# The last modulation's loads and additions at other places within the chunks of the feed-forward

## The chip, the core and the metric

The kernel runs on one core of a Trainium2 chip. Its engines work side by side, each through its own queue of instructions: TensorE (PE in the profile, its weight loads PEld), VectorE (DVE), ScalarE (ACT), GpSimd (POOL) and SyncE (SP), which only starts DMA transfers. The metric is the time of one execution on the device in microseconds (us), as the median of several runs; lower is better.

## The reference

One layer of a diffusion step, for 128 context tokens and 256 latent tokens of width 2048. What bears on the change is the modulation and the feed-forward at the end:

```python
mod = jax.nn.silu(cond) @ lw['w_ada'] + lw['b_ada']
sh1, sc1, ga1, sh2, sc2, ga2 = [m[:, None, :] for m in jnp.split(mod, N_MOD, axis=-1)]
...
x = x + ga1 * rmsnorm(m, lw['norm_post_mix'])
h = rmsnorm(x, lw['norm_pre_ffn']) * (1.0 + sc2) + sh2
ff = (jax.nn.silu(h @ lw['w_ffn_gate']) * (h @ lw['w_ffn_up'])) @ lw['w_ffn_down']
x = x + ga2 * rmsnorm(ff, lw['norm_post_ffn'])
```

`w_ada` has 2048 x 12288 elements, six modulations of 2048 columns. The change concerns the sixth, `ga2`, which is only needed at the very end, for the last line. There are two conditions, one for the context tokens and one for the latent tokens, so each modulation is a product of two vectors with a matrix. The feed-forward has 5632 hidden columns.

## The kernel before

**Numbers.** All is float32. For a product each operand is split into a high part (`whi`, `hid_hi`, a rounded copy made by ScalarE) and a low part (`wlo`, `hid_lo`, the rest, a subtraction on VectorE), and TensorE adds three products: high by high, high by low, low by high. Every weight that comes from memory therefore costs one copy on ScalarE (L1437) and one subtraction on VectorE (L1448) of a 128 x 1024 tile before TensorE can use it.

**Chunks and steps.** The hidden columns are worked through in 11 chunks of 512 (`NFC = 11`, `FC = 4` tiles of 128). Chunk 0 is done plainly. Chunks 1 to 10 use a scheme with seven products in place of eight, for which sums of weights are formed on VectorE: a chunk's gate and up products are the kinds A to H, each in four steps i = 0 to 3 (A0 to A3, B0 to B3, and so on), and the down product of the chunk before is woven in between as DA to DH and D4 to D7. A list `steps`, written out by a loop, sets the order: A0 to A3; B0 to B3; D4; then C and E in turn, with D5, DA, DB and DC behind E0 to E3; then F and G in turn, with DE to DH behind G0 to G3; then H0 to H3, with D6 behind H0 and D7 behind H2. Every step takes one pair of split weight tiles (`whi`, `wlo`) for its matmuls (L1539) and, in `grab2`, has the pair for the third step after it made (`split_next`: the copy L1437, the sums L1420, L1444, L1445 and L1447, the subtraction L1448). There are four buffers each for `whi` and `wlo`.

**What else a step does.** `pend` is a list of small operations that the following steps put into their engines' queues: the hidden activations of the previous chunk (ScalarE's `hid_hi` and VectorE's `hid_lo`, L1630) behind A2, B0 and B2, their sums (L1637 to L1644), and the evictions of finished products. The results of the down products are added to sums in memory by transfers that GpSimd issues (L1672).

**The order.** The queues of TensorE, ScalarE, VectorE and GpSimd hold their instructions in the order in which the program calls them. SyncE's transfers in the loop are placed by a planner. An instruction waits in its queue for what it needs, and everything behind it in that queue waits too.

**The last modulation.** The generator `ada_last` computes it in four quarters `q` of 512 columns. One step of a quarter loads a tile of 128 x 512 of `w_ada` (L1476; 256 KB) into one half of a two-part buffer `w5` and lets VectorE add it, multiplied by one scalar per partition, to an accumulator, once per condition: a plain multiplication for the first tile (L1479), a multiply-add for the other fifteen (L1481). After the sixteenth step `turned` is set. Two further steps, at A0 and A1 of the next chunk, sum over the partitions with small matmuls (L1492), turn the result (L1499) and finish the quarter with three short operations on VectorE (L1502 to L1505). The generator is advanced by one step at chosen places, at the end of a step of the main loop:

```python
ada_at = ('B2', 'E0', 'E2', 'F0', 'G1', 'G3', 'H0', 'H2')
...
if (kind == "A" and i < 2) if turned[0] else c < LAST and kind + str(i) in ada_at:
    step(ada)
```

Eight places per chunk make two chunks per quarter: the 64 loads are spread over chunks 1 to 8, and chunk 9 begins with the last two steps of the fourth quarter.

Of the kernel before, what the change touches and what calls it, by code (L numbers as in the profile page):

```python
# [97 lines left out]
def tile_step(ctx: ExitStack, tc: tile.TileContext, a, o):  # L98
# [150 lines left out]
    def step(side):  # L249
        if side is not None:  # L250
            next(side, None)
# [19 lines left out]
    def paced(gen, rate):  # L271

        due = 0.0
        while True:
            due += rate[0]
            while due >= 1.0:
                due -= 1.0
                if next(gen, 1) is not None:
                    return
            yield  # L280
# [766 lines left out]
    with ExitStack() as s:  # L1047
# [84 lines left out]
        E0, S0, S12 = (pss.tile([P, 2, 3, 64], F32, tag="side", name="pst") for _ in range(3))  # L1132
# [208 lines left out]
        LAST = NFC - 1  # L1341
# [117 lines left out]
        def grab2(kept=2):  # L1459
            w = take()  # L1460
            while now:
                now.pop(0)()
            load_more(kept)
            split_next()
            return w


        d_live, turned = [0], [False]
# [50 lines left out]
        for u in range(HEAD):  # L1519
            kind, c, j = ffn_order[u]  # L1520
# [11 lines left out]
        def products(w, todo, by_tile=False):  # L1532

            order = [(x, y) for x in ((0, 1),) for y in todo] if by_tile else [((0,), y) for y in todo] + [((1,), y) for y in todo]
            for ws, (dst, stat, mov, first, last, *more) in order:
                for w_ in ws:
                    for m in range(2):
                        for x_ in range(2 - w_):
                            PE.matmul(  # L1539
                                dst, stat[x_][m], mov(w[w_], m),  # L1540
                                start=first and w_ == m == x_ == 0, stop=last and w_ == m == 1,
                                skip_group_check=any(more),
                            )
# [7 lines left out]
        def two_of(blocks, i):  # L1551
            return [[x[:, 2 * i + m, :] for m in range(2)] for x in blocks]
# [5 lines left out]
        def banks(c):  # L1558

            return dict(zip(("q2", "p2", "Q", "X", "Z"), pgu[:3] + pgu[3 + c % 2 : 4 + c % 2] + pgu[4 - c % 2 : 5 - c % 2]))  # L1560
# [13 lines left out]
        def evict(c, kind):  # L1574

            B = banks(c)
            add, mul = DVE.tensor_add, DVE.tensor_mul
            silu = lambda x, y=None: ACT.activation(x, x if y is None else y, AF.Silu)
            if kind == "A":
                now.extend([lambda: ACT.copy(sq, B["Q"]), lambda: ACT.copy(s1, B["X"])])  # L1580
            elif kind == "B":
                now.append(lambda: ACT.copy(s5, B["Z"]))
            elif kind == "C":
                now.append(lambda: silu(g0, B["Q"]))
            elif kind == "E":
                now.append(lambda: ACT.copy(e2, B["X"]))
                pend.extend([lambda: add(g1, e2, B["Z"]), lambda: silu(g1)])
            elif kind == "F":
                pend.extend([lambda: add(s5, s5, B["X"]), lambda: silu(s5)])
            elif kind == "G":  # L1590
                pend.extend([
                    lambda: add(s1, s1, B["p2"]), lambda: mul(g1, g1, s1),
                    lambda: add(sq, sq, B["q2"]), lambda: mul(g0, g0, sq),
                ])
            elif kind == "H":
                pend.append(lambda: mul(s5, s5, B["X"]))
# [67 lines left out]
        def to_sums(k, p, c):  # L1664

            u = dt["out"][turn[0] % 4]
            turn[0] += 1
            ACT.copy(u, p)  # L1668
            if c == 0:
                SP.dma_start(sums_d[k], u)  # L1670
            else:
                POOL.dma_start(sums_d[k], u, accum_op=ALU.add)  # L1672
            d_live[0] -= 1
# [11 lines left out]
        def sums_join(at):  # L1685

            for x, y in (
                ("q2", "q1"), ("q3", "q1"), ("p2", "p1"), ("p6", "p1"), ("p3", "p5"), ("p3", "p6"), ("p7", "p6"),
                ("p5", "p7"), ("p4", "p7"),
            ):  # L1690
                pend.append(lambda x=at[x], y=at[y]: DVE.tensor_add(x, x, y))
# [19 lines left out]

        rate[0] = 1.0
        ada = paced(ada_last(), rate)
        ada_at = ('B2', 'E0', 'E2', 'F0', 'G1', 'G3', 'H0', 'H2')
        pd_tiles, hid_last, x1b, done = None, None, None, 0
        d_bank, late_w = {}, []
        for kind, c, i in steps:
# [54 lines left out]
            elif kind[0] == "D":  # L1772
                w = grab2()
                while pend:
                    pend.pop(0)()
                todo = []
                for n, stat, first, last in of_d[kind]():
                    if first:
                        d_bank[n] = psm.tile([P, 512], F32, tag="mm", name="pds")
                        d_live[0] += 1  # L1780
                    todo.append((d_bank[n], stat, mov_d, first, last))
                    if last:
                        pend.append(lambda k=PROD.index(n), p=d_bank[n], c=c: to_sums(k, p, c))
                products(w, todo, by_tile=kind in ("DB", "DC"))
            else:
                w = grab2()
                if kind == "H" and i == 0:
                    while pend:
                        pend.pop(0)()
                B = banks(c)  # L1790
                products(
                    w, [(B[n], two_of(stat, i), mov_gu, first and i == 0, i == 3, not first) for n, stat, first in of_kind[kind]],
                    by_tile=(kind, i) in (("A", 3), ("B", 0), ("B", 3), ("C", 0)),
                )
                if i == 3:
                    evict(c, kind)
                if (kind, c, i) == ("C", LAST, 0):
                    sums_join(back)
                if (kind, c, i) == ("F", LAST, 0):
                    sums_rest()  # L1800
                if (kind, c, i) == ("B", LAST, 0):
                    while pend:
                        pend.pop(0)()
                    back = sums_back()
                if kind == "A" and i:
                    if c == 1 and i == 2:
                        while pend:
                            pend.pop(0)()
                        d_tiles()
                        load_more()  # L1810
                    if c == 1 and i == 2:
                        f = dt["full"]
                        pend.append(lambda: DVE.tensor_add(f, hid[0][:, :, P:T].bitcast(F32), hid[1][:, :, P:T].bitcast(F32)))
                        pend.extend(hid_sums(f[:, :, 0:P], f[:, :, P:]))
                    if i == 3 and c == 1:
                        pend.append(hid_sums_lo)
                if c > 1 and (kind, i) == ("A", 0):
                    mid = dt["out"][turn[0] % 4]
                at = kind + str(i)
                if c < LAST:  # L1820
                    if at == "H0":
                        pend.append(apart(g1, e2, g1))
                    elif at == "H1":
                        pend.append(apart(g0, sq, g0))
                if c > 1:
                    if at == "A0":
                        pend.append(apart(s5, mid, s5))
                    elif at == "A1":
                        pend.append(together(g1, e2))
                    elif at == "A2":  # L1830
                        pend.extend(hid_parts(1, e2))
                    elif at == "A3":
                        pend.append(together(g0, g1))
                    elif at == "B0":
                        pend.extend(hid_parts(0, g1))
                    elif at == "B1":
                        pend.append(together(s5, mid))
                    elif at == "B2":
                        pend.extend(hid_parts(2, mid))
                        if c < LAST:  # L1840
                            pend.extend(hid_sums(*(x.rearrange("p (j c) -> p j c", j=FC) for x in (e2, mid))))
                    elif at == "B3":
                        if c < LAST:
                            pend.append(hid_sums_lo)
                if (kind == "A" and i < 2) if turned[0] else c < LAST and kind + str(i) in ada_at:
                    step(ada)
            if (kind, c, i) == ("D", NFC - 2, 3):
                while pend:
# [174 lines left out]
```

## Time and profile before

| | |
|---|---|
| median of 3 runs | 1940.47 us (1938.39 to 1945.57) |
| the profiled execution, its own time | 1937.62 us |
| its span, from the first to the last instruction | 1935.8 us |
| feed-forward, chunks 1 to 9 (start of A0 of chunk 1 to start of A0 of chunk 10) | about 968 to 1794 us |
| granted TensorE clock, mean over the span | 0.998 |

A row of the order-of-time view gives start, length, engine, line, operation, what it writes and reads, shapes, and the count where equal neighbours are merged; in brackets stands how long the engine was idle before it and what ended that idle time. A row of the waits view reads "who waited <- for whom: us in total, times, longest". Letters such as `u`, `raw`, `dw` and `spare` are buffers. PE's instructions overlap: the length of one is more than the distance between two starts.

### The profile page before, as it was taken

The page shows a single profiled execution, that of the slowest core. Times are in us where ns is not written, and L with a number is a line of the kernel's source. Part 1 is how long each engine was busy: PE and PEld are TensorE (multiplying, and loading weights), DVE is VectorE, ACT ScalarE, POOL GpSimd, SP SyncE. Part 2 cuts the span into 40 slices and gives each one's busy share as a digit, 9 for nine tenths or more (in the row PEclk, how much of TensorE's full clock was granted, in tenths as well). Part 3 has the DMA queues.
Part 4 walks back from the last instruction along what each step waited for, and adds up shares of the span by engine and source line. Part 5 has one row for each costly group of instructions (what it writes and reads, how often), then busy time and mean ns, then how long its engine had stood idle before and what let it go on. Part 6 is the DMA issues. An engine that isn't in the chain of part 4 may idle for free.

```text
span 1935.8 us, 27972 instructions
## 1 busy us (share of the span) xinstructions
PE 1920.4 (99%) x10398; PEld 1703.5 (88%) x10398; DVE 1638.8 (85%) x2059; ACT 1069.1 (55%) x1523; POOL 145.2 (8%) x171
## 2 busy tenths in 40 slices
PE   8999999999999999999999999999999999999998
PEld 6779999999999999999988888888888888888886
DVE  5569888879776787977799999999999998998885
ACT  4233454554335655446456666666666666666554
POOL 0000000000000000003000111111111120211001
PEclk9999999999999999999999999999999999999999
DMA  9977777767754687754639596969888797969563
GB/s 390 373 261 265 232 253 226 236 220 255 257 194 142 205 285 245 220 185 158 224 102 297 122 285 152 266 161 249 195 239 208 211 236 181 247 153 253 158 204 123
DMA packets 246152, 429.12 MB, mean 222 GB/s; under 512 B 45308, under 2 KB 149948, under 8 KB 241664
## 3 DMA queue, kind: packets, MB, share of 16 engines
q1 hardware_dynamic: 199072, 386.70, 60.3%
q0 software_dynamic: 18432, 33.56, 11.1%
q10 hardware_dynamic: 28512, 7.08, 2.5%
q8 instruction: 81, 1.33, 0.3%
q14 instruction: 55, 0.45, 0.1%
HBM read 365.68 MB, written 54.53 MB: 217 GB/s over the span
## 4 chain that ended last, share of the span: by engine, by line
PE 95%; DVE 2%; DMA 2%; ACT 1%; issue 1%; SPq 0%; POOL 0%; DVEq 0%; ACTq 0%; POOLq 0%
PE pmm L257 35%; PE pgu L1539 30%; PE pdn L1539 10%; PE pds L1539 7%; PE pv L399 3%; PE pgm L382 1%; PE pf L998 1%; PE px L417 1%; PE pmm L1253 1%; PE bk L1539 1%; PE po L647 1%; PE pf L999 0%; DMA xraw<-in_w_x 0%; DMA Clo<-in_xT 0%; DMA raw<-in_w_br_gla 0%
## 5 line engine op out<-in xcount | busy, mean ns | idle before, releaser
L257 PE MATMUL pmm<-A_hi,whi 128*128 128x384 f32 x1200 | 404.3, 337 | 0.0
L257 PE MATMUL pmm<-A_hi,wlo 128*128 128x384 f32 x1200 | 401.4, 334 | 0.0
L257 PE MATMUL pmm<-A_lo,whi 128*128 128x384 f32 x1200 | 401.3, 334 | 0.0
L1437 ACT CAST whi<-u 128x1024 fp32r<-128x1024 f32 x200 | 210.1, 1055 | 179.3 <-DVE u L1444 42.3
L223 ACT CAST whi<-raw 128x1024 fp32r<-128x1024 f32 x181 | 190.3, 1054 | 185.8 <-DMA raw<-in_w_gate 54.4
L224 DVE TENSOR_TENSOR wlo<-raw,whi 128x1024 fp32r<-128x1024 f32 x179 | 218.4, 1222 | 57.4 <-ACT whi L223 57.0
L1448 DVE TENSOR_TENSOR wlo<-u,whi 128x1024 fp32r<-128x1024 f32 x200 | 242.9, 1222 | 17.9 <-ACT whi L1437 17.5
L1539 PE MATMUL pgu<-whi,A_hi 128*128 128x512 f32 x640 | 250.0, 391 | 0.0
L1539 PE MATMUL pgu<-whi,A_lo 128*128 128x512 f32 x640 | 249.2, 389 | 0.0
L257 PEld LDWEIGHTS pmm<-A_hi,whi 128*128 128x128 f32 x1200 | 225.3, 188 | 2.9 <-issue 1.4
L257 PEld LDWEIGHTS pmm<-A_lo,whi 128*128 128x128 f32 x1200 | 225.4, 188 | 0.2
L257 PEld LDWEIGHTS pmm<-A_hi,wlo 128*128 128x128 f32 x1200 | 225.2, 188 | 0.0
L574 DVE SCALAR_TENSOR_TENSOR adacc<-adaw,cond,adacc 128x1024 f32<-128x1024 f32 x180 | 222.9, 1281 | 2.7 <-DMA adaw<-in_w_ada 2.4
L1437 ACT CAST whi<-raw 128x1024 fp32r<-128x1024 f32 x157 | 165.2, 1054 | 83.0 <-PE pdn L1539 22.7
L1448 DVE TENSOR_TENSOR wlo<-raw,whi 128x1024 fp32r<-128x1024 f32 x157 | 191.8, 1222 | 8.9 <-ACT whi L1437 8.6
L1539 PE MATMUL pgu<-wlo,A_hi 128*128 128x512 f32 x640 | 185.8, 389 | 0.0
L1539 PEld LDWEIGHTS pgu<-whi,A_hi 128*128 128x128 f32 x640 | 120.1, 188 | 26.1 <-issue 0.8
L1539 PEld LDWEIGHTS pgu<-wlo,A_hi 128*128 128x128 f32 x640 | 120.2, 188 | 25.1
L1539 PEld LDWEIGHTS pgu<-whi,A_lo 128*128 128x128 f32 x640 | 120.2, 188 | 24.7
L1539 PE MATMUL pgu<-whi,S 128*128 128x512 f32 x400 | 116.6, 389 | 0.0
L1672 POOL DMA_DIRECT2D sums_d<-spare x64 | 58.6, 950 | 622.5 <-ACT spare L1668 616.1
L1539 PE MATMUL pdn<-whi,hid_lo 128*128 128x512 f32 x264 | 102.9, 390 | 0.5 <-DVE hid_lo L1630 0.5
(410 smaller groups left out, 3308.0 us busy)
## 6 DMA issues: line engine op xcount, KB each, us to landing
adaw<-in_w_ada SPq DMA_DIRECT2D x96, 512.0 KB, 4.4
raw<-in_w_d SPq DMA_DIRECT2D x70, 512.0 KB, 6.3
slab<-in_w_ada SPq DMA_DIRECT2D x32, 1024.0 KB
raw<-in_w_gate SPq DMA_DIRECT2D x64, 512.0 KB, 4.5
raw<-in_w_g SPq DMA_DIRECT2D x48, 512.0 KB, 3.7
raw<-in_w_u SPq DMA_DIRECT2D x48, 512.0 KB, 5.0
raw<-in_w_in SPq DMA_DIRECT2D x44, 512.0 KB, 4.2
u<-in_w_u SPq DMA_DIRECT2D x40, 512.0 KB, 6.1
```

The source lines that it names most:

```text
L223: ACT.copy(hi, raw)
L224: sub = lambda: eng.tensor_sub(lo, raw, hi.bitcast(F32))
L257: PE.matmul(dst, w[wi][:, k * n + n0 : k * n + n0 + P], x[xi][:, k0 + k, :], start=first and k == 0 and j == 0, stop=last and k == kts - 1 ...
L382: PE.matmul(pgv[q : q + 32, :], spad[:, k, :], slab[k // (KT // 2)][:, k % (KT // 2), :], start=k < 4, stop=k >= KT - 4,)
L399: PE.matmul(pv[2 * t + g], hT[x_][:, kb, t * P : (t + 1) * P], w_[:, g * 512 : (g + 1) * 512], start=kb == 0 and j == 0, stop=kb == KT - 1 ...
L417: PE.matmul(px, w_[:, u * P : (u + 1) * P], hT[x_][:, kb, :], start=j == 0, stop=j == 2)
L574: DVE.scalar_tensor_tensor(acc[:, c, :], w, cond[:, k, c : c + 1], acc[:, c, :], op0=ALU.mult, op1=ALU.add,)
L647: PE.matmul(dst, w[wi], x[xi], start=first and j == 0, stop=last and j == 2)
L1437: ACT.copy(hi, src)
L1448: DVE.tensor_sub(lo, src, hi.bitcast(F32))
L1539: PE.matmul(dst, stat[x_][m], mov(w[w_], m), start=first and w_ == m == x_ == 0, stop=last and w_ == m == 1, skip_group_check=any(more),)
L1672: POOL.dma_start(sums_d[k], u, accum_op=ALU.add)
```

## The change

One tuple becomes two, and the one that holds is chosen by the chunk's number: the first for chunk 1, the second for the chunks from 2 on. Each has eight places, as before.

```diff
-        ada_at = ('B2', 'E0', 'E2', 'F0', 'G1', 'G3', 'H0', 'H2')
+        ada_at = (('B0', 'B2', 'E0', 'E2', 'F0', 'G1', 'G3', 'H0'), ('A2', 'B0', 'B2', 'E0', 'E2', 'F0', 'G3', 'H1'))
...
-                if (kind == "A" and i < 2) if turned[0] else c < LAST and kind + str(i) in ada_at:
+                if (kind == "A" and i < 2) if turned[0] else c < LAST and kind + str(i) in ada_at[c > 1]:
                     step(ada)
```

In chunk 1 the place B0 is new and H2 is gone. In the later chunks A2, B0 and H1 are new, and G1, H0 and H2 are gone. The generator, its loads and its operations are the same.

## The prediction

> **What bounds the kernel now.** I read the page's head first, then the chain of waits, then the waits and the stretches of the feed-forward, and last the order of time on VectorE inside one chunk.
>
> ```profile
> span 1935.8 us, 27972 instructions
> PE 1920.4 (99%) x10398; PEld 1703.5 (88%) x10398; DVE 1638.8 (85%) x2059; ACT 1069.1 (55%) x1523; POOL 145.2 (8%) x171
> PE 95%; DVE 2%; DMA 2%; ACT 1%; issue 1%; SPq 0%; POOL 0%; DVEq 0%; ACTq 0%; POOLq 0%
> ```
>
> TensorE (PE) is busy for 99% of the span and carries 95% of the chain that ended last. The page is an average over stages, so the stage of the change has to be read alone: chunks 1 to 9 of the feed-forward, 968 to 1793 us. One row of the stretches view is one chunk (columns: length; busy time and count of PE, PEld, DVE, ACT, POOL; granted clock; DMA share; GB/s):
>
> ```profile
> 1059.70:1151.80 92.10, 91.59 (x403) 75.32 (x403) 87.02 (x91) 58.81 (x72) 11.54 (x13) 1.00 0.78 208
> 1243.90:1335.00 91.10, 91.10 (x403) 75.47 (x402) 87.06 (x91) 60.17 (x74) 14.02 (x18) 1.00 0.87 216
> 1427.20:1518.20 91.00, 91.00 (x403) 75.39 (x402) 86.22 (x90) 60.78 (x74) 14.11 (x18) 1.00 0.84 219
> ...
> PEld pdn L1539 <- DVE hid_lo L1630: 1.2, 2, 0.9
> PE pdn L1539 <- DVE hid_lo L1630: 0.5, 1, 0.5
> PEld pgu L1539 <- DVE wlo L1448: 0.2, 1, 0.2
> ```
>
> Chunks 4 and 6 hold some 402 matmuls in 91.1 us, 0.227 us each, the granted clock at 1.00 and PE busy throughout. Chunk 2 has the same count in 92.1 us. The last three rows are all that TensorE and its weight loads wait for VectorE in the stage (total, times, longest). So the stage stands at TensorE's own beat, and the only time in it that a better order on VectorE could return is the 1.0 us of chunk 2. VectorE, at 87 of 91.1 us, has little room: it is the engine that could become the bound.
>
> **The change, part by part.** No instruction is added or removed. A step is one load of 256 KB and two instructions on VectorE:
>
> ```profile
> L1481 DVE SCALAR_TENSOR_TENSOR acc<-w,cond,acc x120: 743/750/760, 1000.4 to 1701.8; 128x512 f32<-128x512 f32 x120
> L1476 SPq DMA_DIRECT2D w<-in_w_ada x64: 328/341/1746, 914.1 to 1690.1; - x64
> L1479 DVE TENSOR_SCALAR acc<-w,cond x8: 482/484/489, 992.8 to 1540.3; 128x512 f32<-128x512 f32 x8
>   DMA w<-in_w_ada: 11.3, 8
> DMA to landing us min/median/max: 2.6/5.5/11.0
> ```
>
> 64 loads and 128 instructions (120 of 750 ns, 8 of 484 ns) at eight places a chunk fill chunks 1 to 8 both before and after; chunk 9 only finishes the last quarter. In chunk 1 the place H2 goes and B0 comes. In chunks 2 to 8 the places G1, H0 and H2 go and A2, B0 and H1 come. What counts is therefore where 7 x 3 pairs of instructions stand in VectorE's order. Chunk 4, VectorE alone, at A and B (start, length, idle before):
>
> ```profile
> 1251.82 1.23 DVE L1448 TENSOR_TENSOR wlo<-u,whi 128x1024 fp32r<-128x1024 f32 x1
> 1254.51 0.69 DVE L1630 TENSOR_TENSOR hid_lo<-ep,hid_hi 128x512 fp32r<-128x512 f32 x1 [1.46 <-ACT hid_hi L1630]
> ...
> 1256.25 2.44 DVE L1448 TENSOR_TENSOR wlo<-u,whi 128x1024 fp32r<-128x1024 f32 x2
> 1260.14 0.69 DVE L1630 TENSOR_TENSOR hid_lo<-ep,hid_hi 128x512 fp32r<-128x512 f32 x1 [1.46 <-ACT hid_hi L1630]
> ...
> 1265.29 1.41 DVE L1481 SCALAR_TENSOR_TENSOR acc<-w,cond,acc 128x512 f32<-128x512 f32 x2
> 1266.62 0.69 DVE L1630 TENSOR_TENSOR hid_lo<-spare,hid_hi 128x512 fp32r<-128x512 f32 x1
> ```
>
> *A2 and B0 come.* The step at A2 ends up directly behind the weight split (L1448) that starts at 1251.82, and in front of the hid_lo at 1254.51, which belongs to A3; that at B0 stands in the same way in front of the hid_lo at 1260.14, which belongs to B1. At both places VectorE idles 1.46 us, because ScalarE's hid_hi comes late. A pair occupies 1.41 us and moves the next instruction on by 1.33 (1265.29 to 1266.62). So both pairs fit, with 0.05 to 0.13 us to spare: cost between 0 (all hidden) and 1.33 each (nothing hidden). I take 0, since the idle time is VectorE's own, and ScalarE, not VectorE, ends it. Queued behind these adds are the hid_lo of A3 and B1, and, through B1 to B3, the third hid_lo at 1266.62, for which TensorE waits:
>
> ```profile
> 1267.50 0.19 PEld L1539 LDWEIGHTS pdn<-whi,hid_lo 128*128 128x128 f32 x1
> 1296.51 0.62 PE L1539 MATMUL pds<-wlo,hid_hi 128*128 128x512 f32 x2
> 1294.25 1.23 DVE L1448 TENSOR_TENSOR wlo<-raw,whi 128x1024 fp32r<-128x1024 f32 x1
> 1306.94 0.62 PE L1539 MATMUL pgu<-wlo,A_hi 128*128 128x512 f32 x2
> 1304.72 1.22 DVE L1448 TENSOR_TENSOR wlo<-raw,whi 128x1024 fp32r<-128x1024 f32 x1
> ```
>
> These are the tight spots of chunk 4. The third hid_lo ends at 1266.62 + 0.69 = 1267.31, and its first weight load (of step D 4) starts at 1267.50: 0.19 us of margin. The wlo made in step DB ends at 1295.48 and is used three steps later, in DC, at 1296.51: 1.03. The one made in G0 ends at 1305.94 and is used in G1 at 1306.94: 1.00. If the two pairs keep to their idle time, none of these margins changes. If that cover is gone, the hid_lo in front of D 4 is late first.
>
> *G1, H0 and H2 go, H1 comes.*
>
> ```profile
> 1310.40 1.41 DVE L1481 SCALAR_TENSOR_TENSOR acc<-w,cond,acc 128x512 f32<-128x512 f32 x2
> 1327.53 1.41 DVE L1481 SCALAR_TENSOR_TENSOR acc<-w,cond,acc 128x512 f32<-128x512 f32 x2
> 1332.79 1.42 DVE L1481 SCALAR_TENSOR_TENSOR acc<-w,cond,acc 128x512 f32<-128x512 f32 x2 [0.44 <-DMA w<-in_w_ada]
> ```
>
> These are the three pairs that leave. Behind G1 VectorE runs 1.33 us earlier, behind H0 2.66, behind H1 1.33 again, behind H2 2.66 and the 0.44 us for which it waited there for its load. Here VectorE is packed and its lead is short (1.00 us above), so the relief is real for VectorE; for TensorE it is worth nothing, as no row shows TensorE waiting there. Gain: 0, and it can't be a loss. The lead is carried into A, where ScalarE then starts its weight copies somewhat earlier; that can bring chunk 2's hid_lo forward. I take half of that 1.0 us: between 0 and 1.0 gained.
>
> *The loads.* SyncE issues a load when the step two places earlier has freed its half of the buffer; nothing waits but the adds themselves, and SyncE's queue behind it.
>
> ```profile
> 1322.84 0.76 SPq L1476 DMA_DIRECT2D w<-in_w_ada  x1
> 1328.96 0.34 SPq L1476 DMA_DIRECT2D w<-in_w_ada  x1
> ...
> 1254.00:1266.00 12.00, 12.00 (x55) 9.94 (x54) 10.03 (x11) 10.14 (x13) 0.00 (x0) 1.00 0.35 74
> 1314.00:1326.00 12.00, 12.00 (x55) 9.94 (x54) 11.97 (x15) 9.13 (x12) 2.62 (x3) 1.00 1.08 326
> ```
>
> The adds of H0 end at 1328.94, and the next load leaves at 1328.96. In the new order two loads a chunk leave behind A2 and B0, in a stretch where the DMA engines are 0.35 busy, instead of G and H, where they are full; SyncE's weight loads in G and H are moved past two ada loads fewer. The shortest lead is B2's: its load leaves when A2's adds end, at about 1254.5, and is wanted at 1265.29, 10.8 us later. The slowest of the landings shown took 11.0, the median 5.5. Late by 0.2 at the very worst, which the 0.19 us of margin cover: 0. Every other load has a longer stretch of the order before it.
>
> *Chunk 1.* One pair stands ahead of its old place from B0 to H2, so VectorE is 1.33 us later there.
>
> ```profile
> 1028.45 1.23 DVE L1448 TENSOR_TENSOR wlo<-raw,whi 128x1024 fp32r<-128x1024 f32 x1
> 1031.63 1.07 PE L1539 MATMUL pgu<-wlo,A_hi 128*128 128x512 f32 x4
> ```
>
> The wlo made in its G0 ends at 1029.68 and is used at 1031.63: 1.95 us of margin where chunk 4 has 1.00, more than the 1.33 taken from it: 0.
>
> **A rule of the skill beside it.** The rows of the chunks have weight loads busy for 75.4 of 91.1 us, 83%. The Trainium skill (Perfetto Trace Analysis, Identifying the Most-Contended Engine) says that matmul busy time is a bad measure of TensorE's distance from its limit, and that LDWEIGHTS busy % and MFU are the measures to use. By it TensorE would have 17% left in this stage, and VectorE, at 95%, would be the engine to relieve; relief would shorten the chunk. By the rows of waits it would not. That is the rival "faster" below, which is worked out from rows.
>
> **The sum.** 0 (A2, B0) + 0 (G1, H0, H2, H1) + 0 (loads) + 0 (chunk 1) - 0.5 (chunk 2's stall, between 0 and 1.0) = -0.5 us. The profiled execution took 1937.62 us, 1.8 more than its span, and would become 1937.1. It lies 2.85 below the median of the runs shown, within their spread (1938.39 to 1945.57 among the three). The same difference from the median: 1940.47 - 0.5 = 1940.0.
>
> **The rivals.**
>
> *Slower: the idle time does not take the pairs.*
>
> ```profile
> ACT whi L1437 <- DVE u L1420: 22.3, 15, 3.6
> ACT whi L1437 <- PE pgu L1539: 58.3, 69, 2.5
> ```
>
> Place: the hid_lo of A3 and B1. If the wait for hid_hi moves with VectorE (the first row: ScalarE's weight copies wait for the sums that VectorE makes at A), each pair delays all that follows by 1.33 us, until G1's absence gives it back. Price where the margin is 0.19: one pair not hidden 1.33 - 0.19 = 1.14 us a chunk, x 7 = 8 us, 1948.5; both 2.66 - 0.19 = 2.47, x 7 = 17 us, 1957.5. It decides from a delay of 0.19 us at B1. For it: pairs of 1.41 in gaps of 1.46. Against it: VectorE arrives at A up to 2.66 us earlier, which widens the gaps.
>
> *Faster: TensorE's beat hides waits for VectorE.* If what lies between weight loads is lateness of VectorE, the relief of three pairs, 4.0 us a chunk, x 7 = 28 us, would show: 1912.5. Against it: chunk 6, with 0.84 us less work on VectorE than chunk 4, keeps the same beat to 0.1 us.
>
> *It changes nothing at all.* VectorE's lead is lost again at A, where ScalarE's copies wait for TensorE to free weight buffers (the second row), and chunk 2 keeps its 1.0 us: 1940.5. That is within what I call no change.
>
> **How the numbers follow.** Chances: forecast 0.70, nothing at all 0.13, one pair exposed 0.05, both exposed 0.08, faster 0.04. A measurement of this kernel can't tell under 0.5%, 9.7 us, from no change. So faster 0.04; slower 0.08 (both pairs exposed, +17); within 0.5% the rest, 0.88. The time is that of the forecast, 1940.0. The range goes from 1935 (the lowest run shown, 1938.39, less the 1.0 of chunk 2 and less again the 2.1 by which it lies under the median) to 1949 (one pair exposed, 1948.5, which also holds the slowest run shown). It leaves out the two ends, 0.12.
>
> **What will show it.** Right: the rows of chunks 4 and 6 stay at 91.0 to 91.1 us with 403 matmuls; the idle time before L1630, [1.46 <-ACT hid_hi L1630], shrinks to 0.1 or so at A3 and B1, or grows by VectorE's lead less 1.33; the wait for w in front of L1481, 11.3 us in 8 times, all but goes; chunk 2 comes to between 91.1 and 92.1. Wrong: a chunk of over 92 us in chunks 4, 6 or 8; waits of TensorE for hid_lo or wlo above the 1.9 us shown; or a span shorter by more than 2 us, which would mean that TensorE's beat was not its own.

## The result, and the profile after

The changed kernel takes 1936.42 us in the median of 22 runs (1935.94 to 1940.94); the kernel before takes 1941.11 in 22 runs on the same chip (1936.19 to 1945.57). The ratio is 0.9979, 95% interval [0.9972, 0.9985]: about 4 us faster by the ratio, less than the 0.5% that the prediction called no change, but clear of 1, and eight times the 0.5 us that it forecast. The profiled execution of the changed kernel took 1936.08 us. It stands close to its median; the one of before, 1937.62, was 3.5 us below the median of its 22 runs.

The changed kernel's page, its head and the chain that ended last:

```profile
span 1934.3 us, 27954 instructions
...
PE 97%; DMA 1%; DVE 1%; ACT 0%; issue 0%; SPq 0%; POOL 0%; DVEq 0%; POOLq 0%; ACTq 0%
```

Its stretches view for chunks 2 and 4, with the columns as in the prediction:

```profile
1059.70:1151.80 92.10, 92.10 (x408) 76.27 (x407) 88.34 (x92) 61.80 (x74) 13.02 (x16) 1.00 0.83 229
1243.90:1335.00 91.10, 91.10 (x404) 75.43 (x403) 87.32 (x91) 60.49 (x73) 14.00 (x18) 1.00 0.88 216
```

TensorE's part of the chain rises from 95 to 97%. Chunk 4 has one recorded matmul more than before in the same 91.1 us: its beat is untouched. In chunk 2 TensorE is now busy for all of the stretch (91.59 before) and fits 408 matmuls where 403 stood, since the stall of 1.0 us is gone and the next chunk's start moves into the window. Its waits over the feed-forward from chunk 1 on (960 to 1890 us, chunks 1 to 10; total, times, longest):

```profile
ACT whi L1437 <- DVE u L1420: 10.6, 8, 2.7
DVE hid_lo L1630 <- ACT hid_hi L1630: 8.0, 8, 1.5
PEld pgu L1539 <- DVE wlo L1448: 0.2, 1, 0.2
```

And its order of time in chunk 4, on VectorE at A and B, and the weight load of D4 that takes the third hid_lo:

```profile
1250.85 1.41 DVE L1481 SCALAR_TENSOR_TENSOR acc<-w,cond,acc 128x512 f32<-128x512 f32 x2
1252.40 0.69 DVE L1630 TENSOR_TENSOR hid_lo<-ep,hid_hi 128x512 fp32r<-128x512 f32 x1
...
1256.92 1.41 DVE L1481 SCALAR_TENSOR_TENSOR acc<-w,cond,acc 128x512 f32<-128x512 f32 x2
1258.46 0.69 DVE L1630 TENSOR_TENSOR hid_lo<-ep,hid_hi 128x512 fp32r<-128x512 f32 x1
...
1264.94 0.68 DVE L1630 TENSOR_TENSOR hid_lo<-spare,hid_hi 128x512 fp32r<-128x512 f32 x1
...
1266.71 0.19 PEld L1539 LDWEIGHTS pdn<-whi,hid_lo 128*128 128x128 f32 x1
```

The two new pairs stand where VectorE was idle for 1.46 us: a pair starts 1.55 us before the hid_lo behind it (1252.40 - 1250.85), of which 1.41 are the pair. The third hid_lo ends at 1265.62 (1264.94 + 0.68) and is taken at 1266.71: its margin in front of D4 is 1.09 us where the prediction read 0.19. ScalarE's wait for VectorE's sums (L1420) falls from 22.3 to 10.6 us. No row has VectorE waiting for `w` any longer (11.3 us before), and none has TensorE or its weight loads waiting for hid_lo.

Where did it begin? At the end of chunk 1. The kernel before, in order of time, with rows of SyncE's queue, VectorE, ScalarE and TensorE's weight loads:

```profile
1051.79 0.64 SPq L1476 DMA_DIRECT2D w<-in_w_ada  x1
...
1058.78 1.42 DVE L1481 SCALAR_TENSOR_TENSOR acc<-w,cond,acc 128x512 f32<-128x512 f32 x2 [2.71 <-DMA w<-in_w_ada]
...
1062.98 1.22 DVE L1420 TENSOR_TENSOR u<-u,u 128x1024 f32<-128x1024 f32 x1
...
1064.29 1.06 ACT L1437 CAST whi<-u 128x1024 fp32r<-128x1024 f32 x1 [3.62 <-DVE u L1420]
...
1071.32 1.06 ACT L1580 COPY ep<-pgu 128x512 f32<-128x512 f32 x2
...
1071.94 0.19 PEld L1539 LDWEIGHTS pgu<-whi,A_hi 128*128 128x128 f32 x1 [0.23 <-ACT ep L1580]
...
1084.31 0.19 PEld L1539 LDWEIGHTS pdn<-whi,hid_lo 128*128 128x128 f32 x1 [0.93 <-DVE hid_lo L1630]
```

And the changed kernel in the same view, at the places of the first sum, of the copy behind it and of the first eviction:

```profile
1060.69 1.22 DVE L1420 TENSOR_TENSOR u<-u,u 128x1024 f32<-128x1024 f32 x1
...
1062.00 1.05 ACT L1437 CAST whi<-u 128x1024 fp32r<-128x1024 f32 x1 [1.06 <-DVE u L1420]
...
1069.61 0.59 ACT L1580 COPY ep<-pgu 128x512 f32<-128x512 f32 x1 [0.50 <-PE pgu L1539]
```

Read downwards: before, VectorE waits 2.71 us at H2 of chunk 1 for a tile of `w_ada`, so its first sum of chunk 2 comes at 1062.98; after, at 1060.69, 2.29 us earlier. ScalarE's weight copy, which waits for that sum, moves from 1064.29 to 1062.00, the same 2.29. ScalarE's evictions of A's product (L1580) move from 1071.32 to 1069.61; now they wait for TensorE, where before TensorE's weight load in B0 waited 0.23 us for them. The third hid_lo comes early enough too, and D4's 0.93 us are gone. That is one chain of lateness with two places at which it can stop TensorE, B0 and D4.

### The profile page after: what moved, and what is told of

Read it like the earlier page. It is cut to its first block, busy times and chain, and to the rows that moved or that the text cites. A ratio compares the mean times of both kernels' runs of the same rounds, so it can differ in the third digit from the quotient of the medians.

```text
span 1934.3 us, 27954 instructions
## 1 busy us (share of the span) xinstructions
PE 1918.5 (99%) x10398; PEld 1702.5 (88%) x10398; DVE 1641.8 (85%) x2059; ACT 1069.3 (55%) x1523; POOL 145.2 (8%) x171
## 3 DMA queue, kind: packets, MB, share of 16 engines
q0 software_dynamic: 18432, 33.56, 11.3%
q8 instruction: 81, 1.33, 0.3%
## 4 chain that ended last, share of the span: by engine, by line
PE 97%; DMA 1%; DVE 1%; ACT 0%; issue 0%; SPq 0%; POOL 0%; DVEq 0%; POOLq 0%; ACTq 0%
PE pmm L257 36%; PE pgu L1539 31%; PE pdn L1539 10%; PE pds L1539 7%; PE pv L399 3%; PE pgm L382 1%; PE pf L998 1%; DMA slab<-in_w_ada 1%; PE px L417 1%; PE pmm L1253 1%; PE pf L999 1%; PE bk L1539 1%; PE po L647 1%; PE pr L582 0%; PE dl L647 0%; PE pp L881 0%
## 5 line engine op out<-in xcount | busy, mean ns | idle before, releaser
L1539 PE MATMUL pdn<-whi,hid_hi 128*128 128x512 f32 x264 | 102.8, 389 | 0.0
```

The lines of the kernel that those rows point to most:

```text
L1539: PE.matmul(dst, stat[x_][m], mov(w[w_], m), start=first and w_ == m == x_ == 0, stop=last and w_ == m == 1, skip_group_check=any(more),)
```

## The experiments

The runs below were made on three chips, and each is compared with the kernel before on its own: its median there is 1939.21 us for the first four runs, 1940.65 for the next four and 1939.92 for the last four. In the first four runs chunk 1 keeps its old order, and one place is moved in chunks 2 to 8. The rows of waits are again those from chunk 1 on, 960 to 1890 us. A profile shows one execution only; those of the runs with A2 and with B3 are the fastest of their runs, so they show less than the usual stalls.

**H2 to A2.** The second tuple becomes

```diff
- ... 'H0', 'H2')
+ ('A2', 'B2', 'E0', 'E2', 'F0', 'G1', 'G3', 'H0')
```

> Only one place of the old order is changed, for chunks 2 to 8: H2 becomes A2 (chunk 1 keeps the old order). Theory 1, VectorE's lateness at H2 (the pair there and the wait for its load, up to 2.7 us in the profile of before) is carried through A and B to the third hid_lo of B3, which TensorE needs in step D 4, more so in some executions than in the profiled one: the pair leaves the late stretch and lies in the idle time of A2, so D 4 stalls go, most of the gain comes back: 1936.5 to 1938. Theory 2, the tight weight splits in G (1.0 us of margin) are what executions lose time at: H2 stands behind G, its place doesn't matter there, no gain: 1940 to 1941. Theory 3, the difference lies in the end of the program and not in the chunks: no gain.

Measured: 1940.33 us (1937.65 to 1943.02), ratio 1.0004 [0.9996, 1.0013]: no gain. The wait for `w` at H2 is gone from chunks 2 to 8, and TensorE still waits. Its waits:

```profile
PEld pdn L1539 <- DVE hid_lo L1630: 1.6, 2, 1.0
DVE acc L1481 <- DMA w<-in_w_ada: 2.4, 1, 2.4
DVE u L1420 <- DMA u<-in_w_g: 3.3, 3, 2.2
```

The 2.4 is chunk 1's. The third row is new. In order of time, a load of gate weights in SyncE's queue and VectorE's sum that waits for it, in chunk 4 of this run:

```profile
1241.24 0.37 SPq L1414 DMA_DIRECT2D u<-in_w_g  x1
...
1256.08 1.23 DVE L1420 TENSOR_TENSOR u<-u,u 128x1024 f32<-128x1024 f32 x1 [2.23 <-DMA u<-in_w_g]
```

The load at the same place in the changed kernel:

```profile
1236.92 0.37 SPq L1414 DMA_DIRECT2D u<-in_w_g  x1
```

A wait for another transfer has taken the place of the one removed. In the changed kernel, where G1's and H0's pairs have gone too, that load leaves some 4 us earlier and nobody waits for it.

**H0 to B0.** The second tuple is `('B0', 'B2', 'E0', 'E2', 'F0', 'G1', 'G3', 'H2')`.

> Only one place of the old order is changed, for chunks 2 to 8: H0 becomes B0. Theory 1: VectorE comes to A 1.33 us earlier, but H2 with its wait for the load stays, so a part of the gain: 1937 to 1939.5. Theory 2: nothing in G is relieved, since B0 stands ahead of it: no gain or up to 1 us slower. Theory 3: no gain.

Measured: 1939.52 us (1938.23 to 1940.93), ratio 0.9999 [0.9990, 1.0007]: no gain. Its waits:

```profile
PEld pgu L1539 <- ACT ep L1580: 2.1, 2, 1.2
PEld pdn L1539 <- DVE hid_lo L1630: 1.2, 2, 0.9
DVE acc L1481 <- DMA w<-in_w_ada: 3.7, 1, 3.7
```

H2 in chunk 1 waited 3.7 us here, and TensorE stood in B0 and at D4. The 3.7 is the only wait for `w` left in chunks 1 to 8: the seven others that the kernel before has are gone, and that gave nothing.

**B2 to B3**, behind the third hid_lo instead of in front of it: the second tuple is `('B3', 'E0', 'E2', 'F0', 'G1', 'G3', 'H0', 'H2')`.

> The pair that stands directly ahead of the third hid_lo (place B2) is put behind it (B3), in chunks 2 to 8; all other places are the old ones, H2 and its wait among them. Theory 1: the margin of the third hid_lo grows by 1.33 us in each chunk, so the stalls in D 4 go although VectorE is late as before: 1936.5 to 1938. Theory 2: the margins in G are the same, no gain. Theory 3: no gain.

Measured: 1939.51 us (1936.42 to 1943.46), ratio 1.0003 [0.9995, 1.0012]: no gain. In its waits nothing on TensorE waits for hid_lo any more, but one weight load waits for the eviction:

```profile
PEld pgu L1539 <- ACT ep L1580: 0.8, 1, 0.8
```

This cures D4 alone. B0 is the other place where the same lateness stops TensorE. The pair at B3 has a price of its own: weight loads now wait for `wlo` for 0.3 and 0.4 us in total (`pds` and `pgu`), where the kernel before has 0.2.

**G1 to H1**, so that three pairs stand at H0, H1 and H2: `('B2', 'E0', 'E2', 'F0', 'G3', 'H0', 'H1', 'H2')`.

> Only one place of the old order is changed, for chunks 2 to 8: G1 becomes H1, which relieves G alone by 1.33 us and leaves VectorE's position at H2 and A as it was. Theory 1: no gain, 1940 to 1942, or slightly slower since the pair at H2 then waits longer. Theory 2: the whole gain, 1936.5 to 1938. Theory 3: no gain.

Measured: 1959.09 us (1957.71 to 1961.95), ratio 1.0098 [1.0085, 1.0111]: some 19 us slower, where slightly slower at most was expected. Its waits:

```profile
DVE acc L1481 <- DMA w<-in_w_ada: 30.2, 15, 4.5
PEld pgu L1539 <- ACT ep L1580: 17.0, 8, 3.0
ACT whi L1437 <- DVE u L1420: 44.5, 20, 5.4
```

And VectorE in order of time, at H1 and H2 of chunk 3:

```profile
1247.51 1.42 DVE L1481 SCALAR_TENSOR_TENSOR acc<-w,cond,acc 128x512 f32<-128x512 f32 x2 [1.66 <-DMA w<-in_w_ada]
1251.50 1.41 DVE L1481 SCALAR_TENSOR_TENSOR acc<-w,cond,acc 128x512 f32<-128x512 f32 x2 [1.44 <-DMA w<-in_w_ada]
```

A load may leave only when the pair two places earlier is done. With three places close together in H the loads have too little lead, VectorE waits at two of them in nearly every chunk, and TensorE waits in B0 eight times. This is the same chain made large: waits for `w` at the end of a chunk, 30.2 us where the kernel before has 11.3, cost the next chunk its start.

**A2 and B0 for H0 and H2, G1 kept** (chunks 2 to 8; chunk 1 old): `('A2', 'B0', 'B2', 'E0', 'E2', 'F0', 'G1', 'G3')`.

> Chunks 2 to 8: H0 and H2 become B0 and A2 together, G1 stays (the change but for G1 to H1); chunk 1 in the old order. Theory 1, in the form that the four runs before leave it: in H VectorE waits for the load of H2 (1 to 3.7 us) and is late, ScalarE's copies wait for VectorE's sums at A, and TensorE then waits at one of two places, B0 (for ScalarE's eviction L1580) or D 4 (for the third hid_lo L1630); each single move cured one place or half the lateness, both moves together cure both: 1936 to 1937.5, and all margins at B0 of chunks 3 to 8 at 1.93 us. Rival, the relief of G1 is needed too: 1938.5 to 1940.

Measured: 1937.26 us (1936.06 to 1941.79), ratio 0.9986 [0.9977, 0.9995]: part of the gain at least. The wait at H2 of chunk 1 is there, 3.0 us long, and by the waits TensorE stops twice, both times in chunk 2:

```profile
PEld pdn L1539 <- DVE hid_lo L1630: 0.9, 1, 0.9
PEld pgu L1539 <- ACT ep L1580: 0.5, 1, 0.5
DVE acc L1481 <- DMA w<-in_w_ada: 3.0, 1, 3.0
```

From chunk 3 on no weight load waits for hid_lo or for the eviction: with both new places, VectorE is back in step within one chunk.

**No wait at H2.** The old order, but the eighth and the sixteenth tile of each quarter are loaded and not used: the adds read the tile before once more, which is already there.

```diff
  SP.dma_start(w, ...)
+ if k % 8 == 7:
+     w = wt[:, (k - 1) % 2, :]
```

> The old order, but the additions at H2 use the tile of the step before once more in place of their own, so that they don't wait for their load; the load is still made, and all instructions and transfers are the same in number. It leaves the eighth and the sixteenth tile of each quarter out of the sum. Theory 1 (the wait at H2 is where the lateness comes from): 1936.5 to 1938, and margins at B0 and D 4 like those of the changed kernel but for the pairs' own 2.66 us. Rival A, the pairs in H themselves make VectorE late: 1939 to 1941. Rival B, the DMA engines are full at H and A, and ScalarE waits for its transposes: 1939 to 1941.

Measured: 1936.23 us (1935.64 to 1937.80), ratio 0.9979 [0.9970, 0.9988]. Without moving a single pair, and with all loads still made, the whole gain is there, and in its profile TensorE waits neither for hid_lo nor for the eviction.

**Chunk 1 alone.** Chunk 1 has the new order, chunks 2 to 8 the old one.

```diff
+ ada_at = (('B0', 'B2', 'E0', 'E2', 'F0', 'G1', 'G3', 'H0'), ('B2', 'E0', 'E2', 'F0', 'G1', 'G3', 'H0', 'H2'))
```

> Chunk 1 in the new order (H2 becomes B0), the other chunks in the old one. Theory 1: the wait at H2 of chunk 1 is the longest (2.4 to 3.7 us), and chunk 2's stalls come from it; these go, 0.7 to 1.9 us less, 1937.5 to 1939. Rival, chunk 1 plays no part: as before.

Measured: 1936.08 us in the median (1935.55 to 1938.96, one of 11 executions, 2111.32, apart), ratio 0.9975 [0.9966, 0.9984]: the whole gain from one chunk, better than was expected. By its waits, H2 of the seven later chunks still waits, and TensorE waits neither for hid_lo nor for the eviction:

```profile
DVE acc L1481 <- DMA w<-in_w_ada: 6.9, 7, 1.4
```

That profile is of an execution of 1938.96 us, well above the median. What it lost, it lost outside these chunks. From the first weight load of hid_lo in D6 of chunk 1 to the same one of chunk 9 it takes 732.96 us (1049.42 to 1782.38), and so does the changed kernel (1047.65 to 1780.61). The first of the two comes 1.8 us later than there, and the stretch behind the second is 1.1 us longer. So the time of one execution does not tell by itself whether the chunks stalled.

**The kernel before, once more**, for a second profile of it.

> The kernel before once more, for a second profile of it. Theory 1: if its time lies above 1938, the excess over 1934.5 of span is the sum of stalls at B0 (L1580) and D 4 (L1630), in other chunks than in the first profile. Rival, the excess lies outside chunks 2 to 9.

Measured: 1938.69 us, one execution. Its waits:

```profile
PEld pdn L1539 <- DVE hid_lo L1630: 2.8, 3, 1.5
PEld pgu L1539 <- ACT ep L1580: 0.5, 1, 0.5
DVE acc L1481 <- DMA w<-in_w_ada: 11.7, 8, 3.0
```

And in order of time, VectorE's wait in chunk 4 and the weight load of D4 behind it:

```profile
1256.93 1.23 DVE L1420 TENSOR_TENSOR u<-u,u 128x1024 f32<-128x1024 f32 x1 [0.72 <-DMA u<-in_w_g]
...
1269.17 0.19 PEld L1539 LDWEIGHTS pdn<-whi,hid_lo 128*128 128x128 f32 x1 [1.51 <-DVE hid_lo L1630]
```

The weight loads waited 3.3 us here, against 1.2 + 0.2 in the first profile of the same kernel. Chunk 4, undisturbed in the first profile, makes most of the difference. Between the two weight loads of D6 named above pass 735.75 us (1047.47 to 1783.22), in the first profile 734.01 (1047.50 to 1781.51): the stalls cost 2.79 and 1.05 us beside the 732.96 of the changed kernel. So one profile of this kernel does not show what it usually loses.

**Only the wait at H2 of chunk 1 removed.** The old order everywhere; only the eighth tile of the first quarter is left out in the manner above.

```diff
+ if (q, k) == (0, 7):
+     w = wt[:, 0, :]
```

> The old order everywhere; only at H2 of chunk 1 the additions use the tile of the step before once more, so that they don't wait for their load (the eighth tile of the first quarter is left out of the sum). Theory 1, as the runs so far leave it: the wait of 2.7 to 3.0 us at this one place makes VectorE late for chunk 2, and the old order, with VectorE nearly full, carries the lateness from chunk to chunk: 1936 to 1937.5, the whole gain. Rival, the pair at H2 of chunk 1 itself (1.33 us) has to go from there: 1938 to 1941.

Measured: 1936.83 us (1935.88 to 1937.72), ratio 0.9983 [0.9973, 0.9992]: as expected. One wait out of eight carries most or all of the gain. In its profile chunk 2 has no stall left; one is left at D4 of chunk 4 (0.9 us), behind a wait of VectorE for gate weights of 0.7.

**Chunk 1 alone, made late again.** The chunk-1-only order, with three extra pairs of adds behind the eighth tile of the first quarter, at H2 of chunk 1 (that tile then counts four times; 'H2' is added to chunk 1's places for them).

```diff
+ if (q, k) == (0, 7):
+     for c in (0, 1) * 3:
+         DVE.scalar_tensor_tensor(acc[:, c, :], w, cond[:, k, c : c + 1], acc[:, c, :], ...)
+     yield
```

> The kernel with the new order in chunk 1 alone (1936.1), and at its H2 three more pairs of additions of the eighth tile (six instructions, 4.0 us of VectorE's time, the pair of 1.33 and the wait of 2.7 that stood there before; the tile counts four times in the sum). Theory 1, VectorE's lateness is the cause, whatever makes it: the time goes back to that of the kernel before, 1939 to 1941.5, with stalls at B0 and D 4 in chunk 2 and later ones. Rival, the place of chunk 1's loads in SyncE's queue is the cause: it stays at 1936 to 1937.

Measured: 1938.83 us (1937.27 to 1944.18), ratio 0.9998 [0.9988, 1.0008]: the gain is gone. In order of time on VectorE, the added work:

```profile
1058.37 4.06 DVE L1488 SCALAR_TENSOR_TENSOR acc<-w,cond,acc 128x512 f32<-128x512 f32 x6
```

And the waits, where the added lines shift the numbers (L1586 is the eviction, L1636 the hid_lo):

```profile
PEld pgu L1545 <- ACT ep L1586: 1.4, 1, 1.4
PEld pdn L1545 <- DVE hid_lo L1636: 0.9, 1, 0.9
```

4.06 us of work in the place of the old pair and its wait (1.33 + 2.71) bring back both stalls in chunk 2. The load of H2 is not there to be late, so it is VectorE's lateness that stops TensorE, whatever makes it.

**The changed kernel, made late in the same way.**

> The changed kernel with the same three pairs more at H2 of chunk 1 (the tile counts four times in the sum). Theory 1: the new order of chunks 2 to 8 takes up the lateness within one chunk, in the idle time at A2 and B0 and in the relief of H: stalls in chunk 2 alone, 0.8 to 1.8 us, 1937 to 1938. Rival, the places in chunks 2 to 8 don't matter for catching up: as much lost as with the old ones there, 1939 to 1941.5.

Measured: 1938.74 us (1938.11 to 1940.98), ratio 0.9994 [0.9985, 1.0003]; the profile has the same two stalls in chunk 2 (1.3 and 0.9) and no other. The new places were to catch up where the old ones can't. The two medians are 0.1 us apart, so this pair does not show it; in both profiles chunk 2 alone pays (735.05 and 735.01 us between the two weight loads of D6). The spread differs (2.9 us here, 6.9 in the run before), which hints at it and no more.

**The changed kernel, once more.**

> The changed kernel once more, beside the three on the same chip: 1936 to 1937 by both theories.

Measured: 1936.53 us (1935.45 to 1939.70), ratio 0.9980 [0.9970, 0.9991], on another chip than the first time: the gain repeats.

## Why the prediction was right or wrong

**The forecast as a whole.** 1940.0 was said, 1936.42 came, inside the range and inside 0.5%. The mechanism that it named as its only gain, VectorE's lead carried into A, ScalarE's copies earlier, chunk 2's hid_lo earlier, is the one in the rows. Its source was not: the lead that reaches A of chunk 2 comes from the end of chunk 1, while the prediction took it from G1, H0 and H2 of chunks 2 to 8, which stand behind that stall. The size was wrong too. That the time falls inside is in part luck: the low end of the range, 1935, was made from the lowest run shown and the spread of the runs, not from a larger price of the stalls.

**The step that failed** is the term for chunk 2's stall, -0.5 (0 to 1.0). It was read from one execution. That execution's stall is indeed gone. But the second profile of the same kernel lost 3.3 us where the first lost 1.4, and the kernel's times spread over 9.4 us (1936.19 to 1945.57) while 20 of the changed kernel's 22 lie within 1.6 (1935.94 to 1937.51). The profiled execution, 1937.62, was a mild one; the prediction noted that it lay below the median and then took its stalls for those of the median. By the times the kernel's usual loss is about 4 us; the two profiles show 1.05 and 2.79 of it in the chunks. No profile at or above the median of before was caught, so the rest of it is not shown in any trace.

**"Chunk 1: 0"** failed with it. The question asked there was whether the new pair at B0 does harm. It does none. What was not asked is what the pair that goes leaves behind: H2 of chunk 1 held the longest of the eight waits for `w`, 2.71 of the 11.3 us, just ahead of the chunk that stalls. Removing that wait gives 0.9983, reordering chunk 1 alone 0.9975, putting work in its place 0.9998.

**G1, H0 and H2 go, H1 comes: 0** holds for chunks 2 to 8 where VectorE is in step. Chunk 1's order alone gives 0.9975 [0.9966, 0.9984], the full change 0.9979 [0.9972, 0.9985]. The later chunks' new order without chunk 1's was not run as it stands; the nearest run keeps G1. Where VectorE is late the later chunks' order does count: with the wait in chunk 1 kept, A2 and B0 together, G1 kept, give 0.9986. The two halves of the change are two cures for one loss, and do not add up.

**A2 and B0: 0** is right. The 1.46 us of idle time took the pairs of 1.41. That no margin would change was too low: the one in front of D4 went from 0.19 to 1.09 us in chunk 4.

**The loads: 0** is right for the change as it is; the wait for `w` is gone altogether. The direction of the danger is shown by the run with G1 at H1: three places close together in H cost 19 us.

**The rivals.** *Idle time does not take the pairs*: no; TensorE waits less. *TensorE's beat hides waits*: no. Chunk 4 keeps its 91.1 us. The rule of the Trainium skill that was weighed there (Perfetto Trace Analysis, Identifying the Most-Contended Engine) would have left TensorE 17% to gain. With all waits of VectorE for loads and all of TensorE's for hid_lo removed, the weight loads are still busy for 75.43 of 91.1 us, and the chunk is no shorter. *Nothing at all* is refused by the interval.

**"What will show it."** All four signs of "right" came. The bound on the other side, a span shorter by more than 2 us, was not crossed: 1935.8 to 1934.3. That hangs on the executions caught: from the second profile of before (1936.9) it would have been 2.6 us. Nor would crossing it have spoken against TensorE's beat, since stalls that go shorten the span as well.

**What stays open.** In which chunk the lateness stops TensorE changes from execution to execution. In chunk 4 a late load of gate weights stood ahead of D4's stall in three of the runs above (with A2, the second profile of before, and chunk 1's wait alone removed), but why that load lands late in some of them is not settled: 9 of the 14 profiles have no such wait. Nor is it settled why the two kernels with three extra pairs agree, or what makes the parts outside the chunks vary; up to the first of the two weight loads of D6 the profiles of before (1047.50 and 1047.47) and of the changed kernel (1047.65 and 1047.02) do not differ in a way that could explain the gain.

## What to carry to other kernels

Before a stall is priced, take several profiles of the kernel before, or compare the profiled time with the median and the spread: a profiled execution well below the median shows only part of the losses. When a piece of work is moved, price the wait that it leaves behind as well as the room where it goes, chunk by chunk; a total over eight chunks hid the one wait that counted. And on an engine that is 95% busy a wait of 3 us is not over when it ends: it comes out one chunk later, at another engine's instruction, and sometimes at a different one each time.

## What the runs showed of the hardware

**A load can be late though its buffer is free.** VectorE finished with this half of the buffer at G3 of chunk 1, whose last add, the first row below, ends at 1046.55. The tile for H2 left SyncE at 1051.79, behind these:

```profile
1045.79 0.76 DVE L1481 SCALAR_TENSOR_TENSOR acc<-w,cond,acc 128x512 f32<-128x512 f32 x1
...
1047.50 0.34 SPq L1670 DMA_DIRECT2D sums_d<-spare  x1
1048.18 0.37 SPq L1414 DMA_DIRECT2D dw<-in_w_d  x1
1049.63 2.10 SPq L1414 DMA_DIRECT2D u<-in_w_g  x2
1051.79 0.64 SPq L1476 DMA_DIRECT2D w<-in_w_ada  x1
```

That is 5.2 us behind other transfers, some of which wait for buffers of their own (between 1036 and 1062 us the loads of L1414 waited 4.5 us for VectorE's `wlo`), and 7.0 more until VectorE could start on the tile at 1058.78 (the median from issue to landing of all 64 loads of `w` is 5.5). VectorE was ready at 1056.07 (1058.78 - 2.71). Had the load left when its half came free, the same 7.0 would have ended at 1053.55; this is an estimate, and no run moved that load alone.

**A wait comes out late and elsewhere.** The 2.71 us of VectorE at 1056.07 show at TensorE as 0.23 us at 1071.94 and 0.93 at 1084.31, up to 28 us later, at instructions that wait for ScalarE's eviction and for another of VectorE's products. The view of waits names those two, and not the load.
